# Mixture b's projections read in token order, and the sample's dilated keys kept by residue of four, in a hybrid encoder layer

## The chip, the cores and the metric

One core of a Trainium2 chip runs the whole program. The metric is the device time of one execution in microseconds; lower is better. Three runs of the kernel before took 2401.13, 2403.4 and 2403.99 us; their median is 2403.4 us.

## What is computed

One layer of a bidirectional encoder runs on two requests that share the weights: a prompt of 512 tokens and a sample of 1024, both of width 1024.

```python
x = layer_norm(x)
# token_mixer
q, k, v of a and b = split(x @ w_in)          # 2 x 8 heads of 64
oa = dilated_mixture_attention(rotary(qa), rotary(ka), va)  # windows (128, 1), (512, 4), (2048, 16), merged by lse
ob = neighbourhood_attention(qb, kb, vb, rpb) # tokens as a grid of rows x 64; window 8 x 16, bias by offset
x = layer_norm(ALPHA * x + concat(rmsnorm(oa), rmsnorm(ob)) @ w_out)
x = layer_norm(ALPHA * x + cross_attention(x, mem))   # 4 heads of 256, 256 memory tokens
x = layer_norm(ALPHA * x + relu(x @ w_up)**2 @ w_down)
```

Everything is fp32. The kernel splits each operand of a product into a high part that TensorE multiplies fast and a rest, and adds three products (hi x hi, hi x lo, lo x hi).

## The kernel before

The stages follow one another: keys and values of the memory and the first layer norm (to about 112 us), the prompt's mixture a (112 to 219) and b (219 to 349), the sample's mixture a (349 to 603) and b (603 to 829), then `w_out`, cross-attention and the MLP of both requests to the end. The normalised activations stay in SBUF transposed, features on partitions, as tiles of 8 x 512 tokens: `x0h`/`x0l` are the prompt's high and low parts, `x1` and `x2` the two groups of the sample.

`mixer(r, fill)` (L258) does the mixtures of one request. For each of 4 pairs of heads, `pair_ab` (L595 on) makes the queries and keys of the first head for each group of 512 tokens, the values of both heads, then the attention of the first head, the queries and keys of the second, and its attention. A projection (`proj`, L271) is 8 k-tiles x 3 products = 24 matmuls of 128x512 by `mm3` (L125 to 130) into a PSUM bank `pj`. For mixture b the moving operand is read group by group of the 8-column grid (`p (r g c) -> p g r c`), in runs of 8 tokens, so that the product comes out in the order in which neighbourhoods are compact.

In mixture a, `qk_a` (L335) applies the rotary table (DVE L342 to L344, POOL L345), splits the result (ACT L346, DVE L347), and `stack` (L327 to 333) moves queries and keys by six DMAs on SP's queue into a tile `hd`, where one partition half holds high and the other low parts. In mixture b, `qk_b` (L350 to 365) evacuates PSUM straight into `hd`, with the 1/8 of the scores in the queries, and two DMAs (L364, L365) duplicate the keys to the other half.

The attention of half a head (4 blocks of 128 queries) is a generator, `unit` (L420): scores by two matmuls for each block (L450, L451), bias and row maximum on DVE (L430, `soften`), exponential on ACT (L434); then transposes (L476) and their split (L479, L480); then the product with the values (L492) and ACT's evacuation (L498); then the transposes back (L502) and the sum of halves (L505). `push` and `step` advance the units as a pipeline, one step for each new unit. The sample's mixture a (`attn_a1`, L532) has two units of local blocks (keys 64 before to 64 after) and two of dilated blocks, whose queries and keys are read at stride 4 (`cols(..., 4)`).

The order in which each engine runs its instructions is written out by the framework's scheduler, which works from estimated costs; the engines themselves run in order and wait on semaphores. Tiles come from rotating slots: `gb` has two buffers of 1024 values (mask tables, bias windows), `kv` two, `qt` two. The padded bias table of mixture b, `RB`, is built in DRAM in the first stage (L244 to 251).

Of the kernel before, what the change touches and what calls it, by code (L numbers as in the profile page):

```python
# [36 lines left out]
def tile_encoder_layer(ctx: ExitStack, tc: tile.TileContext, d, outs):  # L37
# [10 lines left out]
    vs = [dr.tile([4, P, 2, 2, NMEM], F32, name=f"vs{i}") for i in range(2)]  # L48
    RB = dr.tile([8, 31, 8, 40], F32, name="RB")
# [197 lines left out]
    rp = d["rpb"]  # L247
    for cq in range(8):
        S.dma_start(RB[:, 8:23, cq, 8:32],
                    bass.AP(tensor=rp.tensor, offset=rp.offset + 14 * 31 + 7 - cq,  # L250
                            ap=[[465, 8], [-31, 15], [1, 24]]))
# [6 lines left out]
    def mixer(r, fill):  # L258
# [12 lines left out]
        def proj(w, g, is_b):  # L271
            o = bank("pj")
            rh, rl = ([x[:, k] for k in range(8)] for x in xg[g])
            if is_b:
                rh, rl = ([a.rearrange("p (r g c) -> p g r c", r=8, g=8) for a in q] for q in (rh, rl))
            mm3(o, w[0], w[1], rh, rl)
            return o

# [48 lines left out]
        def stack(hd, sh, sl, tt):  # L327

            qs, k1, k2 = hd
            for o, x, w in ((slice(0, 64), sh, sl), (slice(64, P), sl, sh)):  # L330
                S.dma_start(f32(qs[o, tt]), f32(x[0:P:2]))
                S.dma_start(f32(k1[o, tt]), f32(x[1:P:2]))
                S.dma_start(f32(k2[o, tt]), f32(w[1:P:2]))

        def qk_a(hd, w, g):  # L335
            o = proj(w, g, False)
# [11 lines left out]
            stack(hd, sh, sl, tt)  # L348

        def qk_b(hd, w, g):  # L350
            o = proj(w, g, True)
            qs, k1, k2 = hd
            lo, hi = slice(0, 64), slice(64, P)
            if r:
                part = lambda a: a.rearrange("p (g x) -> p g x", g=8)[:, :, g * 64:(g + 1) * 64]
                o = o.rearrange("p (g x) -> p g x", g=8)
            else:
                part = lambda a: a
            A.activation(part(qs[lo]), o[lo], AF.Copy, scale=0.125)
            A.activation(part(k2[hi]), o[hi], AF.Copy)  # L360
            V.scalar_tensor_tensor(part(qs[hi]), o[lo], 0.125, f32(part(qs[lo])), op0=ALU.mult, op1=ALU.subtract)
            V.tensor_sub(part(k1[hi]), o[hi], f32(part(k2[hi])))
            if g == ng - 1:
                S.dma_start(f32(k1[lo]), f32(k2[hi]))  # L364
                S.dma_start(f32(k2[lo]), f32(k1[hi]))  # L365
# [9 lines left out]
        def v_proj(v, chunk, pair, is_b):  # L375
# [10 lines left out]
            if is_b and r:  # L386
                vt = slot("kv")
                for g in range(ng):
                    o = proj(w, g, is_b)
                    A.activation(vt.rearrange("p (g x) -> p g x", g=8)[:, :, g * 64:(g + 1) * 64],  # L390
                                 o.rearrange("p (g x) -> p g x", g=8), AF.Copy)
                for k in range(2):
                    v_trans(v[k], [vt[:, c * P:(c + 1) * P] for c in range(4 * k, 4 * k + 4)])
                return
            pad = is_b or r
            last = None
            for g in range(ng):
                o = proj(w, g, is_b)
                vt = slot("kv", 640)
                A.activation(vt[:, 64:576], o, AF.Copy)  # L400
# [19 lines left out]
        def unit(hd, v, h, blocks, norm=None, then=None):  # L420


            qs, k1, k2 = hd
            st = sb.tile([P, 16], F32, name="st", bufs=4)
# [3 lines left out]
            def soften():  # L428
                for i, so, p, bias in todo:
                    V.tensor_tensor_reduce(out=p, in0=so, in1=bias, scale=1.0, scalar=LOWEST, op0=ALU.add,  # L430
                                           op1=ALU.max, accum_out=st[:, 8 + i:9 + i])
                    nm, den = st[:, 2 * i + 1:2 * i + 2], st[:, 2 * i:2 * i + 1]
                    V.tensor_scalar(nm, st[:, 8 + i:9 + i], -1.0, None, op0=ALU.mult)  # L433
                    A.activation(p, p, AF.Exp, bias=nm, accum_out=den)  # L434
# [97 lines left out]
        def attn_a1(hd, v, h, tab, hg):  # L532
            for j in range(2):
                bl = []
                for b in range(4 * j, 4 * j + 4):
                    lead, n = (64, 192) if b == 0 else (0, 192) if b == 7 else (0, 256)
                    bl.append((cols(b * P, P), cols(b * P - 64 + lead, n), tab[:, lead:lead + n], n, lead, 256,
                               (b, b + 1 if b < 7 else "tail")))
# [3 lines left out]
                push(unit(hd, v, h, bl, then=then))  # L542
# [35 lines left out]
        def attn_b(hd, v, h, j, bt, ob, then):  # L578
# [11 lines left out]
            push(unit(hd, v, h, bl, norm=ob, then=then))  # L590
# [40 lines left out]
        for is_b in (False, True):  # L631
            tab = tables(is_b)
            for pair in range(4):
# [542 lines left out]
```

## Time and profile before

| | |
|---|---|
| median of three runs | 2403.4 us |
| the profiled execution | 2400.22 us |
| its span | 2398.4 us |
| instructions in the span | 33111 |
| mean granted TensorE clock | 0.991 |

The profile shows one execution. PE is TensorE's matmuls, PEld its weight loads, DVE is VectorE, ACT ScalarE, POOL GpSimd and SP SyncE, which here issues DMAs; SPq marks SP's DMA queue. A row of a timeline gives the start, the recorded time and the instruction, with the idle time before it and what ended it in brackets. Matmuls overlap: the recorded time of one is longer than the distance to the next. "out<-in" are tile names; `hd<-qt` is a DMA from a tile `qt` into `hd`.

### The profile page before, as it was taken

The numbers are of one execution on the slowest core, as the hardware profiler recorded it, in microseconds if no ns is written. First come the engines' busy times: TensorE is split into PE (matmuls) and PEld (weight loads), VectorE is DVE, ScalarE is ACT, GpSimd is POOL, SyncE is SP. The second block draws the span as 40 slices with busy tenths as digits, with TensorE's granted clock in tenths as the row PEclk, the third lists the DMA queues.
The fourth block names the chain that finished last, engine by engine and source line by source line (L and its number), as shares of the span: only waits on it lengthen the run. The fifth ranks groups of instructions, "written<-read, shape, count | busy, mean of one in ns | idle before, by whom it ended". The sixth has DMA issues, their size and how long they took to land. (4 is left out here: it accounts for less than half of the span.)

```text
span 2398.4 us, 33111 instructions
## 1 busy us (share of the span) xinstructions
PE 2313.8 (96%) x11128; PEld 1911.1 (80%) x11128; DVE 1599.5 (67%) x3304; ACT 1028.7 (43%) x2200; POOL 906.0 (38%) x820
## 2 busy tenths in 40 slices
PE   8989999999999999999989999999999999999987
PEld 6877778988888787877868877878888888888865
DVE  6256545666656677668566487767766696686987
ACT  4346644655545544433233333333354322344443
POOL 7555442212234114533244354555541324213142
PEclk9999999999999999999999999999999999999998
DMA  9666345445435543436335444444489999959762
GB/s 323 203 189 178 89 104 136 116 111 120 103 92 128 174 136 98 127 106 198 101 106 175 123 150 150 122 145 137 160 222 210 207 236 241 212 130 199 196 162 73
DMA packets 389210, 370.99 MB, mean 155 GB/s; under 512 B 71984, under 2 KB 301360, under 8 KB 389040
## 3 DMA queue, kind: packets, MB, share of 16 engines
q1 hardware_dynamic: 346032, 335.31, 47.6%
q0 software_dynamic: 43008, 33.56, 9.9%
q8 instruction: 88, 1.44, 0.3%
q14 instruction: 82, 0.67, 0.1%
HBM read 290.75 MB, written 52.97 MB: 143 GB/s over the span
## 5 line engine op out<-in xcount | busy, mean ns | idle before, releaser
L106 POOL TENSOR_TENSOR wl<-wraw,wh 128x512 fp32r<-128x512 f32 x80 | 105.9, 1338 | 183.5 <-ACT wh L105 167.3
L434 ACT ACTIVATE q<-q,st 128x256 f32<-128x256 f32 (+3 forms) x256 | 138.3, 545 | 75.0 <-DVE st L433 72.1
L975 ACT ACTIVATE wh<-q 128x512 fp32r<-128x512 f32 x176 | 110.0, 625 | 132.7 <-DMA q<-in_w_up_dram 84.4
L976 DVE TENSOR_TENSOR wh<-q,wh 128x512 fp32r<-128x512 f32 x176 | 126.3, 720 | 56.8 <-ACT wh L975 56.8
L480 DVE TENSOR_TENSOR pt<-t,pt 128x512 fp32r<-128x512 f32 x160 | 105.3, 670 | 86.8 <-ACT pt L479 86.2
L960 POOL DMA_DIRECT2D q<-in_w_up_dram x64 | 84.1, 1463 | 182.2 <-DVE h L1013 74.8
L298 POOL TENSOR_TENSOR wl<-wraw,wh 128x256 fp32r<-128x256 f32 x128 | 94.2, 759 | 152.6 <-ACT wh L297 145.7
L913 POOL TENSOR_TENSOR wl<-pt,wh 128x512 fp32r<-128x512 f32 x64 | 91.6, 1451 | 119.0 <-ACT wh L912 118.7
L960 POOL DMA_DIRECT2D q<-in_w_down_dram x64 | 56.4, 956 | 203.4 <-DMA q<-in_w_down_dram 92.2
L479 ACT ACTIVATE pt<-t 128x512 fp32r<-128x512 f32 x160 | 89.4, 582 | 87.3 <-PE o L492 83.8
L106 POOL TENSOR_TENSOR wl<-qt,wh 128x512 fp32r<-128x512 f32 x64 | 101.7, 1609 | 51.6 <-ACT wh L105 43.7
L492 PE MATMUL o<-pt,tok 128*128 128x256 f32 (+3 forms) x560 | 114.0, 314 | 5.8 <-ACT q L498 4.1
L118 POOL TENSOR_TENSOR wl<-wraw,wh 128x512 fp32r<-128x512 f32 x48 | 62.3, 1314 | 127.8 <-ACT wh L117 127.8
L926 DVE TENSOR_TENSOR tok<-tok,t 128x512 f32<-128x512 f32 x124 | 82.8, 679 | 37.3 <-PE t L130 37.3
L130 PE MATMUL pj<-x20h,wl 128*128 128x512 f32 x256 | 101.1, 395 | 2.7 <-POOL wl L106 2.4
L926 DVE TENSOR_TENSOR tok<-tok,s 128x512 f32<-128x512 f32 x124 | 83.8, 679 | 29.7 <-PE s L130 29.5
L128 PE MATMUL pj<-x20h,wh 128*128 128x512 f32 x256 | 100.5, 393 | 1.1 <-ACT wh L105 1.0
L129 PE MATMUL pj<-x20l,wh 128*128 128x512 f32 x256 | 100.0, 390 | 0.0
L1055 ACT ACTIVATE wh<-wraw 128x512 fp32r<-128x512 f32 (+2 forms) x96 | 53.1, 557 | 106.9 <-issue 45.5
L476 PE MATMUL t<-ident,q 128*128 128x128 f32 x624 | 95.3, 274 | 2.8 <-ACT q L434 1.4
L105 ACT ACTIVATE wh<-wraw 128x512 fp32r<-128x512 f32 x80 | 48.0, 627 | 104.1 <-DMA wraw<-in_w_xq_dram 27.2
L492 PEld LDWEIGHTS o<-pt,tok 128*128 128x128 f32 x560 | 83.4, 192 | 11.3 <-ACT q L498 6.3
(489 smaller groups left out, 7601.0 us busy)
## 6 DMA issues: line engine op xcount, KB each, us to landing
q<-in_w_up_dram SPq DMA_DIRECT2D x128, 256.0 KB
q<-in_w_down_dram SPq DMA_DIRECT2D x128, 256.0 KB
wraw<-in_w_in_dram SPq DMA_DIRECT2D x96, 256.0 KB
qt<-in_w_up_dram SPq DMA_DIRECT2D x32, 512.0 KB
pt<-in_w_down_dram SPq DMA_DIRECT2D x32, 512.0 KB
q<-in_w_up_dram POOLq DMA_DIRECT2D x64, 256.0 KB, 8.2
q<-in_w_down_dram POOLq DMA_DIRECT2D x64, 256.0 KB, 6.0
sa<-kv SPq DMA_DIRECT2D x28, 512.0 KB
```

The source lines that it names most:

```text
L106: G.tensor_sub(wl[:, sl], r, f32(wh[:, sl]))
L128: T.matmul(out, lh[k], rh[k], start=(k == 0), stop=False, skip_group_check=True)
L129: T.matmul(out, lh[k], rl[k], start=False, stop=False, skip_group_check=True)
L130: T.matmul(out, ll[k], rh[k], start=False, stop=(k == n - 1), skip_group_check=True)
L434: A.activation(p, p, AF.Exp, bias=nm, accum_out=den)
L476: T.transpose(t[:, x:x + P], p, ident)
L480: V.tensor_sub(lo[:, 0:x], t[:, 0:x], f32(hi[:, 0:x]))
L492: T.matmul(o[:, q0:q0 + n], v(c, h), part[:, x:x + n], start=(done == 0 and part is hi), stop=(done == total - 1 and part is lo), skip_gro ...
L926: V.tensor_add(x, x, q)
L960: G.dma_start(out, src, accum_op=ADD)
L975: A.activation(dst[0], x, AF.Copy)
L976: low.tensor_sub(dst[1], x, f32(dst[0]))
```

## The change

Four things change. `proj` reads the tokens of mixture b in their own order, and the evacuations (ACT and DVE in `qk_b`, ACT in `v_proj`) read PSUM by group and write the same places as before. The factor 1/8 of mixture b moves from the queries into the exponential's scale, and the bias table is multiplied by 8 on its way to `RB`, through SBUF and a new DRAM tile `rp`. In the sample's mixture a, `stack` first copies the high keys (ACT) and the low keys (POOL) into a tile `perm` ordered by residue of four, and the key DMAs move those, 64x4x128 in place of 64x512, so that keys of one residue lie side by side in `hd`; the queries stay as they were. Dilated scores then read keys contiguously, local scores read them in four runs, and the local `soften` reads its mask and writes its result at stride 4, which puts the scores back in token order. `perm` lives in the second buffer of `gb`.

```diff
@@ dram tiles, first stage @@
+    rp = dr.tile([8, 15, 31], F32, name="rp")
...
-    rp = d["rpb"]
+
+    z = slot("tok", 465)
+    S.dma_start(z[0:8], d["rpb"][0].rearrange("h r c -> h (r c)"))
+    V.tensor_scalar(z[0:8], z[0:8], 8.0, None, op0=ALU.mult)
+    S.dma_start(rp.rearrange("h r c -> h (r c)"), z[0:8])
     for cq in range(8):
         S.dma_start(RB[:, 8:23, cq, 8:32],
-                    bass.AP(tensor=rp.tensor, offset=rp.offset + 14 * 31 + 7 - cq,
+                    bass.AP(tensor=rp.tensor, offset=rp[0].offset + 14 * 31 + 7 - cq,
                             ap=[[465, 8], [-31, 15], [1, 24]]))
@@ mixer @@
-        def proj(w, g, is_b):
+        def proj(w, g):
             o = bank("pj")
             rh, rl = ([x[:, k] for k in range(8)] for x in xg[g])
-            if is_b:
-                rh, rl = ([a.rearrange("p (r g c) -> p g r c", r=8, g=8) for a in q] for q in (rh, rl))
             mm3(o, w[0], w[1], rh, rl)
             return o
+        def by_group(a):
+            return a.rearrange("p (r g c) -> p g r c", r=8, g=8)
+        def grouped(a, g):
+            if r:
+                a = a.rearrange("p (g x) -> p g x", g=8)[:, :, g * 64:(g + 1) * 64]
+                return a.rearrange("p g (r c) -> p g r c", r=8)
+            return a.rearrange("p (g r c) -> p g r c", r=8, g=8)
...
+        def by_residue(a):
+            return a.rearrange("p (x q) -> p q x", q=4)
+        def residues(a):
+            return a.rearrange("p (q x) -> p q x", q=4)
-        def stack(hd, sh, sl, tt):
+        def stack(hd, sh, sl, g):
             qs, k1, k2 = hd
-            for o, x, w in ((slice(0, 64), sh, sl), (slice(64, P), sl, sh)):
+            tt = slice(g * 512, (g + 1) * 512)
+            kh, kl = sh, sl
+            if r:
+                kh, kl = perm
+                A.activation(residues(kh), by_residue(f32(sh)), AF.Copy)
+                G.tensor_copy(residues(kl), by_residue(f32(sl)))
+                kh, kl = residues(kh), residues(kl)
+                k1, k2 = (residues(k)[:, :, g * P:(g + 1) * P] for k in (k1, k2))
+            else:
+                k1, k2 = k1[:, tt], k2[:, tt]
+            for o, x, y, z in ((slice(0, 64), sh, kh, kl), (slice(64, P), sl, kl, kh)):
                 S.dma_start(f32(qs[o, tt]), f32(x[0:P:2]))
-                S.dma_start(f32(k1[o, tt]), f32(x[1:P:2]))
-                S.dma_start(f32(k2[o, tt]), f32(w[1:P:2]))
+                S.dma_start(f32(k1[o]), f32(y[1:P:2]))
+                S.dma_start(f32(k2[o]), f32(z[1:P:2]))
...
         def qk_b(hd, w, g):
-            o = proj(w, g, True)
+            o = proj(w, g)
...
-            A.activation(part(qs[lo]), o[lo], AF.Copy, scale=0.125)
+            o = by_group(o)
+            part = lambda a: grouped(a, g)
+            A.activation(part(qs[lo]), o[lo], AF.Copy)
             A.activation(part(k2[hi]), o[hi], AF.Copy)
-            V.scalar_tensor_tensor(part(qs[hi]), o[lo], 0.125, f32(part(qs[lo])), op0=ALU.mult, op1=ALU.subtract)
+            V.tensor_sub(part(qs[hi]), o[lo], f32(part(qs[lo])))
...
@@ v_proj @@
-                    A.activation(vt.rearrange("p (g x) -> p g x", g=8)[:, :, g * 64:(g + 1) * 64],
-                                 o.rearrange("p (g x) -> p g x", g=8), AF.Copy)
+                    A.activation(grouped(vt, g), by_group(o), AF.Copy)
...
-                A.activation(vt[:, 64:576], o, AF.Copy)
+                if is_b:
+                    A.activation(grouped(vt[:, 64:576], g), by_group(o), AF.Copy)
+                else:
+                    A.activation(vt[:, 64:576], o, AF.Copy)
@@ unit @@
-        def unit(hd, v, h, blocks, norm=None, then=None):
+        def unit(hd, v, h, blocks, norm=None, then=None, scale=1.0, local=False):
             qs, k1, k2 = hd
+            order, keyed = (by_residue, residues) if local else (lambda a: a, lambda a: a)
...
-                    V.tensor_tensor_reduce(out=p, in0=so, in1=bias, scale=1.0, scalar=LOWEST, op0=ALU.add,
+                    V.tensor_tensor_reduce(out=order(p), in0=keyed(so), in1=order(bias), scale=1.0, scalar=LOWEST, op0=ALU.add,
                                            op1=ALU.max, accum_out=st[:, 8 + i:9 + i])
...
-                    V.tensor_scalar(nm, st[:, 8 + i:9 + i], -1.0, None, op0=ALU.mult)
-                    A.activation(p, p, AF.Exp, bias=nm, accum_out=den)
+                    V.tensor_scalar(nm, st[:, 8 + i:9 + i], -scale, None, op0=ALU.mult)
+                    A.activation(p, p, AF.Exp, bias=nm, scale=scale, accum_out=den)
@@ attn_a1: local=True for the local units @@
-                    bl.append((cols(b * P, P), cols(b * P - 64 + lead, n), tab[:, lead:lead + n], n, lead, 256,
-                               (b, b + 1 if b < 7 else "tail")))
+                    k0 = (b * P - 64 + lead) // 4
+                    bl.append((cols(b * P, P), lambda z, k0=k0, n=n: residues(z)[:, :, k0:k0 + n // 4],
+                               tab[:, lead:lead + n], n, lead, 256, (b, b + 1 if b < 7 else "tail")))
...
-                        bl.append((cols(512 * i + q, P, 4), cols(q, 256, 4),
+                        bl.append((cols(512 * i + q, P, 4), cols(q * 256, 256),
@@ attn_b: scale=0.125; end of mixer @@
             tab = tables(is_b)
+            perm = parts("gb") if r and not is_b else None
```

The scheduler writes a new order. TensorE's rows are the same up to the start of the sample's mixture a, and no row moves in the MLP. Line numbers of the changed kernel are larger: L450/L451 become L481/L482, L128 to L130 L129 to L131, L476 L507, L502 L533, L371 L398, L410 L439, L345 L375, L331 to L333 L361 to L363, L364/L365 L391/L392, L106 L107, L541 L573, L552 L584, L562 L594, L703 L736.

The first place is TensorE in the sample's mixture a, pair 0, between the first head's first local unit and its second. `s<-hd` are scores, `pj<-x2h,wh` a projection, `t<-ident` transposes. Before:

```order
L502 MATMUL t<-ident,q 128x128 x3
L371 MATMUL pj<-ident,kv 128x128 x4
L410 MATMUL pj<-ident,kv 128x128 x4
L502 MATMUL t<-ident,q 128x128
L450 MATMUL s<-hd 128x256 x2
L476 MATMUL t<-ident,q 128x128 x3
L451 MATMUL s<-hd 128x256 x2
L450 MATMUL s<-hd 128x256
L451 MATMUL s<-hd 128x256
```

And now:

```order
L533 MATMUL t<-ident,q 128x128 x4
L398 MATMUL pj<-ident,kv 128x128 x4
L439 MATMUL pj<-ident,kv 128x128 x4
L507 MATMUL t<-ident,q 128x128
L129 MATMUL pj<-x2h,wh 128x512
L130 MATMUL pj<-x2l,wh 128x512
L131 MATMUL pj<-x2h,wl 128x512
```

Seven more such triples follow, and only then `L481 MATMUL s<-hd 128x256`: a whole projection of 24 matmuls has moved ahead of the second group of scores.

The second place is pair 1 in the same stage. TensorE reaches the first scores of the first head (`128x192`), before:

```order
L130 MATMUL pj<-x1h,wl 128x512
L128 MATMUL pj<-x2h,wh 128x512
L129 MATMUL pj<-x2l,wh 128x512
L130 MATMUL pj<-x2h,wl 128x512
L128 MATMUL pj<-x2h,wh 128x512
L450 MATMUL s<-hd 128x192
L450 MATMUL s<-hd 128x256
L129 MATMUL pj<-x2l,wh 128x512
L451 MATMUL s<-hd 128x192
L450 MATMUL s<-hd 128x256
L451 MATMUL s<-hd 128x256 x2
```

And now:

```order
L129 MATMUL pj<-x1h,wh 128x512
L130 MATMUL pj<-x1l,wh 128x512
L131 MATMUL pj<-x1h,wl 128x512
L481 MATMUL s<-hd 128x192
L481 MATMUL s<-hd 128x256
L129 MATMUL pj<-x2h,wh 128x512
L130 MATMUL pj<-x2l,wh 128x512
L131 MATMUL pj<-x2h,wl 128x512
L482 MATMUL s<-hd 128x192
L481 MATMUL s<-hd 128x256
L482 MATMUL s<-hd 128x256 x2
```

The first scores follow the last `x1` matmul at once, where before four `x2` matmuls stood between. Up to the head's second local unit the order before has 23 projection matmuls (20 of `x2`, 3 of `x1`) after the first score, the new one 35 (24 and 11). On POOL the same pair reads, before:

```order
L445 MEMSET q 128x64
L345 TENSOR_TENSOR qt<-qt 128x512
L106 TENSOR_TENSOR wl<-wraw,wh 128x512 x2
L345 TENSOR_TENSOR qt<-qt 128x512 x2
L298 TENSOR_TENSOR wl<-wraw,wh 128x256 x2
L447 MEMSET q 128x64
```

And now:

```order
L375 TENSOR_TENSOR qt<-qt 128x512
L476 MEMSET q 128x64
L355 CAST gb<-qt 128x512
L107 TENSOR_TENSOR wl<-wraw,wh 128x512 x2
L375 TENSOR_TENSOR qt<-qt 128x512
L355 CAST gb<-qt 128x512
L375 TENSOR_TENSOR qt<-qt 128x512
L355 CAST gb<-qt 128x512
```

The copies `L355` of the low keys stand between the rotary sums `L375`, and the weight split `L107` behind the first of them.

The third place is SP's queue at the end of the sample's mixture a. Before:

```order
L541 DMA oas_61<-cpr 128x4x66
L703 DMA qt<-os_59 128x1024
L364 DMA hd<-hd 64x1024
L365 DMA hd<-hd 64x1024
L552 DMA oas_62<-cpr 128x2x66 x4
L562 DMA gb<-RB 128x16x24
```

And now:

```order
L362 DMA hd<-gb 64x4x128
L361 DMA hd<-qt 64x512
L363 DMA hd<-gb 64x4x128 x2
L362 DMA hd<-gb 64x4x128
L736 DMA qt<-os_59 128x1024
L273 DMA gb<-in_c_m_dram 128x896
L391 DMA hd<-hd 64x1024
L392 DMA hd<-hd 64x1024
L584 DMA oas_62<-cpr 128x2x66 x4
L594 DMA gb<-RB 128x16x24
```

The table of mixture b (`in_c_m`), which was loaded before the sample's mixture a began, is now loaded after the last key DMAs and ahead of the key duplicates `L391` and `L392`.

## Rows read from the trace of the kernel before

**Rows 1.** The page: busy time by engine; the chain that ended last.
```profile
PE 2313.8 (96%) x11128; PEld 1911.1 (80%) x11128; DVE 1599.5 (67%) x3304; ACT 1028.7 (43%) x2200; POOL 906.0 (38%) x820
...
PE 36%; DVE 2%; DMA 1%; POOL 1%; issue 1%; ACT 0%; SPq 0%; ACTq 0%; DVEq 0%
```

**Rows 2.** Windows of three stages (window, length, engines' busy us, granted clock, DMA share).
```profile
219.00:349.00 130.00, 125.08 (x651) 100.55 (x650) 64.17 (x209) 75.63 (x199) 59.66 (x94) 0.99 0.37 93
349.00:603.00 254.00, 249.87 (x1467) 223.94 (x1466) 157.51 (x559) 141.44 (x413) 57.06 (x78) 0.99 0.51 122
603.00:829.00 226.00, 225.81 (x1196) 189.30 (x1195) 138.92 (x445) 120.19 (x305) 72.74 (x89) 1.00 0.47 120
```

**Rows 3.** Waits of PE in the sample's mixture a: total, times, longest.
```profile
PE s L450 <- DMA hd<-qt: 3.6, 1, 3.6
```

**Rows 4.** Timeline of PE: a plain projection, first and last matmul (start, us).
```profile
379.19 0.45 PE L128 MATMUL pj<-x2h,wh 128*128 128x512 f32 x1
...
384.49 0.39 PE L130 MATMUL pj<-x2h,wl 128*128 128x512 f32 x1
```

**Rows 5.** Timeline of PE: a projection of the prompt's mixture b, 1st and 23rd.
```profile
291.46 0.47 PE L128 MATMUL pj<-x0h,wh 128*128 128x512 f32 x1
...
297.09 0.43 PE L129 MATMUL pj<-x0l,wh 128*128 128x512 f32 x1
```

**Rows 6.** Timeline of PE: projections of the sample's mixture b, 22 matmuls.
```profile
719.08 0.47 PE L129 MATMUL pj<-x2l,wh 128*128 128x512 f32 x1
...
724.37 0.43 PE L129 MATMUL pj<-x1l,wh 128*128 128x512 f32 x1
```

**Rows 7.** Timeline of PE: local (445) and dilated (453, 454) scores of 128x256.
```profile
445.47 0.28 PE L451 MATMUL s<-hd 128*128 128x256 f32 x1
...
445.72 0.28 PE L451 MATMUL s<-hd 128*128 128x256 f32 x1
...
453.39 0.42 PE L451 MATMUL s<-hd 128*128 128x256 f32 x1
...
453.87 0.42 PE L451 MATMUL s<-hd 128*128 128x256 f32 x1
...
454.37 0.58 PE L450 MATMUL s<-hd 128*128 128x256 f32 x1
```

**Rows 8.** Timeline of PE's weight loads: contiguous queries (445) and strided ones (454).
```profile
445.36 0.19 PEld L451 LDWEIGHTS s<-hd 128*128 128x128 f32 x1
...
454.34 0.31 PEld L450 LDWEIGHTS s<-hd 128*128 128x128 f32 x1
```

**Rows 9.** Timeline of SP: last key DMAs of stacks in pairs 0 and 1.
```profile
372.30 0.58 SPq L333 DMA_DIRECT2D hd<-qt  x1
...
410.07 0.59 SPq L333 DMA_DIRECT2D hd<-qt  x1
...
415.84 0.59 SPq L333 DMA_DIRECT2D hd<-qt  x1
```

**Rows 10.** Timeline of PE: the score groups that these keys release.
```profile
375.44 0.77 PE L450 MATMUL s<-hd 128*128 128x256 f32 x2 [3.58 <-DMA hd<-qt]
...
415.70 0.39 PE L450 MATMUL s<-hd 128*128 128x192 f32 x2
...
421.65 0.40 PE L450 MATMUL s<-hd 128*128 128x256 f32 x2
```

**Rows 11.** Groups by line, sample's mixture a (busy us, mean ns, idle before).
```profile
L430 DVE CUSTOM_DVE_ANT_0 q<-s,gb 128x256 f32<-128x256 f32 (+1 forms) x112 | 40.9, 410 | 14.9 <-PE s L451 14.1
...
L345 POOL TENSOR_TENSOR qt<-qt 128x512 f32<-128x512 f32 x15 | 19.4, 1290 | 84.0 <-DVE qt L344 66.7 <-DMA hd<-qt 17.3
...
L498 ACT ACTIVATE q<-o 128x512 f32<-128x512 f32 x27 | 16.1, 596 | 9.6 <-PE o L492 9.6
```

**Rows 12.** Timeline of SP: the duplicate of keys for mixture b's first head.
```profile
623.67 0.49 SPq L364 DMA_DIRECT2D hd<-hd  x1
```

**Rows 13.** Timeline of PE: mixture b's first scores of the sample.
```profile
645.72 0.36 PE L450 MATMUL s<-hd 128*128 128x256 f32 x1
```

More of the change, by code (lines that the diff above doesn't have):

```diff
@@ L325, in pair_tiles @@
             return hds, v, chunk
-        def stack(hd, sh, sl, tt):
-            qs, k1, k2 = hd
-            for o, x, w in ((slice(0, 64), sh, sl), (slice(64, P), sl, sh)):
+        def by_residue(a):
[3 more added lines that the diff above has]
+        def stack(hd, sh, sl, g):
+            qs, k1, k2 = hd
+            tt = slice(g * 512, (g + 1) * 512)
[9 more added lines that the diff above has]
+            for o, x, y, z in ((slice(0, 64), sh, kh, kl), (slice(64, P), sl, kl, kh)):
                 S.dma_start(f32(qs[o, tt]), f32(x[0:P:2]))
-                S.dma_start(f32(k1[o, tt]), f32(x[1:P:2]))
-                S.dma_start(f32(k2[o, tt]), f32(w[1:P:2]))
+                S.dma_start(f32(k1[o]), f32(y[1:P:2]))
+                S.dma_start(f32(k2[o]), f32(z[1:P:2]))
         def qk_a(hd, w, g):
-            o = proj(w, g, False)
+            o = proj(w, g)
             tt = slice(g * 512, (g + 1) * 512)
@@ L347, in qk_a @@
             V.tensor_sub(sl, t, f32(sh))
-            stack(hd, sh, sl, tt)
+            stack(hd, sh, sl, g)
         def qk_b(hd, w, g):
-            o = proj(w, g, True)
+            o = proj(w, g)
             qs, k1, k2 = hd
             lo, hi = slice(0, 64), slice(64, P)
[L354 to L358, printed above, removed]
-            A.activation(part(qs[lo]), o[lo], AF.Copy, scale=0.125)
+            o = by_group(o)
+            part = lambda a: grouped(a, g)
+            A.activation(part(qs[lo]), o[lo], AF.Copy)
             A.activation(part(k2[hi]), o[hi], AF.Copy)
-            V.scalar_tensor_tensor(part(qs[hi]), o[lo], 0.125, f32(part(qs[lo])), op0=ALU.mult, op1=ALU.subtract)
+            V.tensor_sub(part(qs[hi]), o[lo], f32(part(qs[lo])))
             V.tensor_sub(part(k1[hi]), o[hi], f32(part(k2[hi])))
@@ L388, in v_proj @@
                 for g in range(ng):
-                    o = proj(w, g, is_b)
-                    A.activation(vt.rearrange("p (g x) -> p g x", g=8)[:, :, g * 64:(g + 1) * 64],
-                                 o.rearrange("p (g x) -> p g x", g=8), AF.Copy)
+                    o = proj(w, g)
+                    A.activation(grouped(vt, g), by_group(o), AF.Copy)
                 for k in range(2):
@@ L397, in v_proj @@
             for g in range(ng):
-                o = proj(w, g, is_b)
+                o = proj(w, g)
                 vt = slot("kv", 640)
-                A.activation(vt[:, 64:576], o, AF.Copy)
+                if is_b:
+                    A.activation(grouped(vt[:, 64:576], g), by_group(o), AF.Copy)
+                else:
+                    A.activation(vt[:, 64:576], o, AF.Copy)
                 if pad and last is None:
@@ L536, in attn_a1 @@
                     lead, n = (64, 192) if b == 0 else (0, 192) if b == 7 else (0, 256)
-                    bl.append((cols(b * P, P), cols(b * P - 64 + lead, n), tab[:, lead:lead + n], n, lead, 256,
-                               (b, b + 1 if b < 7 else "tail")))
+                    k0 = (b * P - 64 + lead) // 4
+                    bl.append((cols(b * P, P), lambda z, k0=k0, n=n: residues(z)[:, :, k0:k0 + n // 4],
+                               tab[:, lead:lead + n], n, lead, 256, (b, b + 1 if b < 7 else "tail")))
                 def then(raw, j=j):
                     S.dma_start(oas[0][j * 512:(j + 1) * 512, hg].rearrange("(i p) c -> p i c", p=P), raw)
-                push(unit(hd, v, h, bl, then=then))
+                push(unit(hd, v, h, bl, then=then, local=True))
             for j in range(2):
@@ L589, in attn_b @@
                                (b, b + 1 if b < 3 else "tail")))
-            push(unit(hd, v, h, bl, norm=ob, then=then))
+            push(unit(hd, v, h, bl, norm=ob, then=then, scale=0.125))
         def pair_ab(pair, is_b, tab):
```

## The prediction

> **What bounds the kernel now.** I read the page first: TensorE (PE) is busy for 96% of the span, and in the chain that ended last PE has 36% of the span and no other engine over 2% [rows 1]. The table by stage then shows whether that holds where the change acts: PE is busy 125.08 of 130 us in the prompt's mixture b, 249.87 of 254 in the sample's mixture a and 225.81 of 226 in its mixture b, at a granted clock of 0.99 to 1.00, so the clock has nothing to give. VectorE (DVE), ScalarE (ACT) and GpSimd (POOL) have a third to three quarters of each stage free [rows 2]. The view of waits holds one PE wait of note in the sample's mixture a, 3.6 us for a DMA into `hd` [rows 3]. So a microsecond comes off the end only if PE's own instructions get shorter or that wait goes. PE's timeline tells what one instruction costs: matmuls overlap, so I take the distance between starts, not the recorded duration.
>
> **Projections of mixture b.** A plain 128x512 projection matmul of the sample's mixture a starts every (384.49 - 379.19)/23 = 0.2304 us [rows 4]. The same matmul with the operand read in runs of eight values starts every (297.09 - 291.46)/22 = 0.2559 us in the prompt's mixture b [rows 5] and every (724.37 - 719.08)/21 = 0.2519 us in the sample's [rows 6]. The change leaves the plain read. Count: 4 pairs x 3 projections x 24 matmuls = 288 for the prompt, twice that, 576, for the sample's two groups. Gain: 288 x 0.0255 = 7.3 and 576 x 0.0215 = 12.4, **-19.7 us**. All of it is PE time in stages that PE bounds.
>
> The regrouping moves to the evacuations, which now read PSUM and write SBUF in runs of eight: 4 for each of 8 heads and group (96) and 12 of values, 108. No row shows such an evacuation. From below it is free; from above it doubles, another 0.60 us each by the ACT row [rows 11], and ACT, busy 75.63 of 130 and 120.19 of 226 us [rows 2], takes even the whole 65 us beside PE. I put it at 0. The scale inside Exp adds no instruction, and the table that is multiplied by 8 costs two DMAs and one DVE instruction in the first stage, far ahead of mixture b: 0.
>
> Where PE gets faster, its covers shrink. The sample's mixture b has no idle PE (0.2 us); the prompt's has 4.9, and 7.3 us less work there can uncover between 0 and 7.3. I take **+2**, a quarter, since ACT and DVE are free half of that stage.
>
> **Dilated scores.** Their keys are read at stride 4: 0.24 us from start to start, (453.87 - 453.39)/2, against 0.125 for local scores of the same 128x256, (445.72 - 445.47)/2 [rows 7]. 8 heads x 2 units x 4 blocks x 2 = 128 matmuls lose the stride. The upper bound is thus 128 x 0.115 = 14.7 us. But their stationary operand, the queries, keeps its stride 4, and its weight load takes 0.31 us where a contiguous one takes 0.19 [rows 8]. The load recorded at 454.34 and the start of its matmul, recorded at 454.37 with 0.58 instead of 0.42 us, hence about 0.16 later in truth, lie 0.19 apart [rows 7, 8]. I read this as: a strided load occupies its path for about 0.2 us before the next can follow, and each of these matmuls has a load of its own. So my estimate for the distance afterwards is 0.22 us, and the gain 128 x 0.02 = **-2.6**, between 0 and -14.7.
>
> **Local scores** now read their keys in four runs of 48 or 64. Bounds: 0, and 128 x 0.0255 = 3.3 us if the runs cost what runs of eight cost. Runs this long are nearest to plain: **+0.2**. DVE reads the mask and writes the scores of 64 local blocks at stride 4; even twice 0.41 us each [rows 11] is 26 us more on an engine busy 157.51 of 254 us [rows 2]: 0.
>
> **The wait at the first head.** Before, PE stands 3.58 us until 375.44 because the last key DMA of the second group is issued only at 372.30, 3.1 us earlier [rows 9, 10]. In the changed order 24 matmuls of a projection, 5.5 us, stand ahead of that second score group. The chain to it is longer, too (next part). I take **-2**, between 0 and -3.58.
>
> **The copies by residue.** Each of 16 `stack` calls gets an ACT copy (like the 128x512 ACT row, 0.60 us) and a POOL copy (like `L345`, 1.29; perhaps twice that, 2.6, as its read is strided) [rows 11]; in all 10 to 19 us on ACT and 21 to 42 on POOL, which have 113 and 197 us free in that stage [rows 2]. So the work is hidden, but the latency is not by itself: keys leave for `hd` later. Take pair 1. The last key DMA of its first group is issued at 410.07; by the 3.1 us above it is there at 413.2, and the first score starts at 415.70: 2.5 us of slack. For the second group 415.84 + 3.1 = 418.9 against 421.65: 2.7 [rows 9, 10]. The new order starts the first scores four matmuls sooner (-0.9: slack 1.6) and puts 8 more matmuls in front of the second ones (+1.8: slack 4.5). The copy is late by 1.3 to 2.6; and the buffer is single, so that the second group's copies wait until the first group's key DMAs have been read: 2.6 (copy) + 3.7 (six issues of about 0.6) + 3.1 (landing) = 9.4 us from stack to stack in place of 415.84 - 410.07 = 5.8 [rows 9], 3.6 later. The second group is thus late by 4.9 to 6.2 against 4.5, which is 0.4 to 1.7 us of PE wait in each of pairs 1 to 3, 1.2 to 5.1: **+2**. Queued behind the waiting copies stand, on ACT, the exponentials of the running head, and on POOL two `L107` and the next `L375`; they are part of that price. The pieces of the key DMAs shrink from 2 KB to 512 bytes; no row shows a price for it here, and SP still issues six of them.
>
> **The order on SP.** `perm` takes the second `gb` buffer, so mixture b's table is loaded only when the last key DMAs have read `perm`, and `L391`/`L392` stand behind it. `L364` was issued at 623.67 and the first score that reads its result starts at 645.72 [rows 12, 13]: 22 us of cover for a wait of one landing (3.1 us). 0.
>
> **Sum:** -19.7 + 2 - 2.6 + 0.2 - 2 + 2 = -20.1; against the profiled execution's own 2400.2 us this is 2380.1. That execution lies 3.2 us below the median of the runs shown, so I forecast **2383** for the median. All low ends but that of the dilated scores (it is R1, below) give -19.7 + 0 - 2.6 + 0 - 3.6 + 1.2 = -24.7, 2379; all high ends -19.7 + 7.3 + 0 + 3.3 + 0 + 5.1 = -4.0, 2399, and they hardly fall together.
>
> **Rivals.**
> *Weight loads hide (R1).* Dilated scores fall to 0.125 us and all 14.7 us come off: 2383 - 12.1 = **2371**. For it: loads overlap the matmuls before them. Against: 0.31 us is longer than a whole 0.125 us matmul. [...] Chance 0.15.
>
> *Runs of eight are free (R2).* If the 0.0255 and 0.0215 us come from something else, such as other reads of the same tiles or the stage's traffic, then projections stay as they are and the first two terms fall away: 2400.2 - 2.6 + 0.2 - 2 + 2 = 2397.8, **2401** on the median, no change. [...] Chance 0.07.
>
> *Half given back (R4).* PE runs ahead of the key duplicates and exponentials of mixture b, and half of the 19.7 us turns into waits: 2383 + 9.9 = **2393**. For it: the prompt's stage has no other work to put in, and evacuations get longer in the chain from projection to score. Against: 0.2 us of idle PE in the sample's stage. Chance 0.11.
>
> *The single `perm` buffer chains the stacks (R3), slower.* If the slack that the new order gives is not there, each second score group of all 8 heads waits 6.2 - 2.7 = 3.5 us: 28 us in place of my 2, so 2383 - 2 + 28 = **2409**. It decides from (2408.2 - 2381)/8 = 3.4 us for each head upwards; below that the projections still win. For it: ACT and POOL run in order, so that a copy that waits for a DMA stops the exponentials behind it, too. Against: the second head's stacks are emitted a whole head ahead of their scores, and 35 matmuls instead of 23 now lie between the two groups. Chance 0.07.
>
> **How the numbers follow.** The forecast has 0.60, R1 0.15, R4 0.11, R2 0.07, R3 0.07. A measurement of this kernel can tell about 0.2% (4.8 us) from no change, so "faster" ends at 2398.6 and "slower" begins at 2408.2. Forecast, R1 and R4 are faster, 0.86, less 0.01 for the forecast's own tail. No change gets that 0.01, R2 and 0.01 of R3, whose time is just past the border: 0.09; the rest of R3, 0.06, is slower. The range reaches down to R1, with a few us for its own spread, and up to R4: 2368 to 2397, which leaves out R2, R3 and the tails.
>
> **What would show it.** Right: all projections of mixture b at 0.230 us from start to start; dilated scores at 0.20 to 0.24 with weight loads still at 0.31; no PE wait over 1 us at the first head, and waits of PE for `hd` under 6 us in all of mixture a; evacuations of b up to twice as long with no one waiting. R1 shows as dilated scores at 0.125. R2 shows as projections of b still at 0.25, R4 as PE idle of some 10 us in the two b stages, R3 as ACT or POOL copies that wait for DMAs and PE waits of 3 us for `hd` at most heads. The forecast is wrong if the span of the two b stages does not shrink by 15 us or more.

## The result, and the profile after

Five executions of the changed kernel took 2383.89, 2383.99, 2384.58, 2386.91 and 2394.04 us, median 2384.58; the five of before beside them 2400.26 to 2403.99, median 2401.13. The ratio is 0.9938, with a 95% interval of 0.9921 to 0.9955. The profiled execution took 2383.99 us with a span of 2382.2, 16.2 less than before's. The forecast was 2383.

The page of the changed kernel, beside [rows 1]:

```profile
PE 2293.0 (96%) x11128; PEld 1903.7 (80%) x11128; DVE 1614.3 (68%) x3305; ACT 1044.8 (44%) x2216; POOL 930.9 (39%) x836
```

PE is busy for 20.8 us less; DVE, ACT and POOL for 14.8, 16.1 and 24.9 us more. Three landmarks on PE cut the span into stages: the first projection of the prompt's mixture b, the first of the sample and the last mixer score. Before (start, us recorded):

```profile
218.77 0.41 PE L128 MATMUL pj<-x0h,wh 128*128 128x512 f32 x1
...
349.98 0.48 PE L128 MATMUL pj<-x1h,wh 128*128 128x512 f32 x1
...
843.43 0.28 PE L451 MATMUL s<-hd 128*128 128x256 f32 x1
```

And after:

```profile
219.70 0.40 PE L129 MATMUL pj<-x0h,wh 128*128 128x512 f32 x1
...
344.49 0.48 PE L129 MATMUL pj<-x1h,wh 128*128 128x512 f32 x1
...
824.28 0.28 PE L482 MATMUL s<-hd 128*128 128x256 f32 x1
```

| stretch | before | after | difference |
|---|---|---|---|
| start to the prompt's mixture b | 218.77 | 219.70 | +0.9 |
| prompt's mixture b | 131.20 | 124.80 | -6.4 |
| sample's mixtures a and b | 493.45 | 479.79 | -13.7 |
| the rest, to PE's last matmul | 1544.96 | 1548.00 | +3.0 |

The mixers gave 20.1 us, the sum of the forecast; 3.9 were lost outside them. To see of what the 13.7 are made, I added up, for each kind of matmul between the landmarks, the time from its start to the next start (any wait of the next matmul is in it): projections 279.8 before, 268.6 after (-11.2); scores 74.2 and 71.4 (-2.8); all others together +0.3, in which the old wait of 3.6 us is gone and new ones are added.

Part of the 13.7 is not the change's. In before's profile the clock was low right behind the wait for `hd` that ended at 375.44 [rows 10]:

```profile
375.40:378.80 3.40, 3.36 (x16) 3.39 (x17) 1.70 (x8) 0.00 (x0) 0.00 (x0) 0.50 0.23 58
```

From there to the next projection at 379.19 [rows 4] PE took 3.75 us. The run with the projections alone (below) has the same matmuls behind its own wait for `hd`, at a clock of 1.00, and takes 2.21 us:

```profile
371.69 0.49 PE L472 MATMUL s<-hd 128*128 128x256 f32 x2 [2.35 <-DMA hd<-qt]
...
373.90 0.44 PE L129 MATMUL pj<-x2h,wh 128*128 128x512 f32 x1
```

So about 1.5 of the 13.7 us are a low clock in before's one profile.

The projections of mixture b, prompt (23 matmuls) and sample (22), against [rows 5, 6]:

```profile
290.42 0.48 PE L129 MATMUL pj<-x0h,wh 128*128 128x512 f32 x1
...
295.50 0.39 PE L130 MATMUL pj<-x0l,wh 128*128 128x512 f32 x1
...
703.80 0.48 PE L130 MATMUL pj<-x2l,wh 128*128 128x512 f32 x1
...
708.66 0.39 PE L130 MATMUL pj<-x1l,wh 128*128 128x512 f32 x1
```

(295.50 - 290.42)/22 = 0.231 and (708.66 - 703.80)/21 = 0.231 us: the plain price of [rows 4]. The evacuations by group cost nothing: 0.684 us (DVE) and 0.581 us (ACT) here, 0.684 and 0.584 before; those of the values take 0.587 us in both. ACT and DVE, group by line, sample's mixture b of the changed kernel:

```profile
L388 DVE TENSOR_TENSOR hd<-pj,hd 64x512 fp32r<-64x512 f32 x16 | 10.9, 684 | 11.1 <-ACT hd L387 10.8
...
L386 ACT ACTIVATE hd<-pj 64x512 fp32r<-64x512 f32 x16 | 9.3, 581 | 7.4 <-PE pj L131 7.3
```

Dilated scores with contiguous keys (timeline of PE, against [rows 7]):

```profile
445.90 0.48 PE L481 MATMUL s<-hd 128*128 128x256 f32 x1
446.22 0.39 PE L482 MATMUL s<-hd 128*128 128x256 f32 x1
446.45 0.40 PE L481 MATMUL s<-hd 128*128 128x256 f32 x1
446.68 0.40 PE L482 MATMUL s<-hd 128*128 128x256 f32 x1
```

From the second on they stand 0.23 us apart; over all such scores with a dilated score before and behind them, the mean went from 0.237 to 0.234 us, which is 0.4 us for 128 of them. The first one behind other work gained more. Its distance to the next is 0.32 here, and it was 0.40 before, from this start to the 453.39 of [rows 7]:

```profile
452.99 0.58 PE L450 MATMUL s<-hd 128*128 128x256 f32 x1
```

Summed from start to next start, all 128 dilated scores took 33.6 us before and 31.8 now: the contiguous key operand bought 1.8 us, where both operands contiguous will bring 14.6 (below).

Waits of PE in the sample's mixture a of the changed kernel (us in total, times, longest), against [rows 3]:

```profile
PE t L507 <- ACT q L465: 3.0, 2, 2.6
PE s L481 <- DVE st L461: 1.2, 2, 0.7
PE s L481 <- DMA hd<-gb: 0.2, 1, 0.2
```

The wait for `hd` is down from 3.6 to 0.2 us, but waits of 4.2 us for ACT's exponentials and DVE's bias step stand in its place, 3.7 of them at the same first head (the two longest here; a third of 0.51 us is behind dilated steps):

```profile
368.89 0.33 PE L507 MATMUL t<-ident,q 128*128 128x128 f32 x1 [2.56 <-ACT q L465]
...
376.33 0.36 PE L481 MATMUL s<-hd 128*128 128x256 f32 x1 [0.68 <-DVE st L461]
```

Groups by line of that stage show what got longer there (busy us, mean ns, idle before):

```profile
L461 DVE CUSTOM_DVE_ANT_1 q<-s,gb 128x256 f32<-128x256 f32 x42 | 24.3, 629 | 7.4 <-PE s L482 7.1
...
L461 DVE CUSTOM_DVE_ANT_0 q<-s,gb 128x256 f32<-128x256 f32 x56 | 20.7, 413 | 0.3
...
L354 ACT ACTIVATE gb<-qt 128x512 fp32r<-128x512 f32 x16 | 18.2, 1141 | 2.3 <-DMA hd<-gb 2.0
...
L355 POOL CAST gb<-qt 128x512 fp32r<-128x512 f32 x15 | 16.6, 1104 | 33.5 <-DVE qt L377 24.9 <-DMA hd<-gb 7.3 <-DVE st L464 1.4
```

The local bias step (`L461`, ANT_1) takes 0.629 us where it took 0.41 [rows 11]; the ACT copy takes 1.14 us (I had taken 0.60) and the POOL copy 1.10 (1.3 to 2.6).

**What was lost outside the mixers.** The granted clock of one stretch in the cross-attention of the changed kernel (window, length, busy us by engine, clock, DMA share):

```profile
1231.60:1237.60 6.00, 6.00 (x18) 5.07 (x19) 2.08 (x3) 1.79 (x3) 0.00 (x0) 0.50 0.42 102
```

The clock is 0.50, and matmuls of 512 columns stand 0.43 us apart, where they stand 0.23 apart once it is back at 0.99. It follows a PE wait of 3.08 us; before, a wait of 3.11 us in the same place was followed by 1.00. Ahead of it the same matmuls come 18.9 us earlier than before, behind it 16.1, so 2.8 us were lost there.

### The profile page after: what moved, and what is told of

It is laid out like the page before. It is cut to its first block, busy times and chain, and to the rows that moved or that the text cites. A ratio compares the mean times of both kernels' runs of the same rounds, so it can differ in the third digit from the quotient of the medians.

```text
span 2382.2 us, 33165 instructions
## 1 busy us (share of the span) xinstructions
PE 2293.0 (96%) x11128; PEld 1903.7 (80%) x11128; DVE 1614.3 (68%) x3305; ACT 1044.8 (44%) x2216; POOL 930.9 (39%) x836
## 5 line engine op out<-in xcount | busy, mean ns | idle before, releaser
L107 POOL TENSOR_TENSOR wl<-wraw,wh 128x512 fp32r<-128x512 f32 x80 | 106.0, 1340 | 173.9 <-ACT wh L106 158.5
L107 POOL TENSOR_TENSOR wl<-qt,wh 128x512 fp32r<-128x512 f32 x64 | 101.7, 1609 | 50.8 <-ACT wh L106 42.8
L131 PE MATMUL pj<-x20h,wl 128*128 128x512 f32 x256 | 101.2, 395 | 2.7 <-POOL wl L107 2.4
L129 PE MATMUL pj<-x20h,wh 128*128 128x512 f32 x256 | 100.6, 393 | 0.3 <-ACT wh L106 0.2
L130 PE MATMUL pj<-x20l,wh 128*128 128x512 f32 x256 | 100.0, 391 | 0.0
L507 PE MATMUL t<-ident,q 128*128 128x128 f32 x624 | 95.2, 273 | 5.0 <-ACT q L465 3.6
L106 ACT ACTIVATE wh<-wraw 128x512 fp32r<-128x512 f32 x80 | 47.7, 626 | 103.5 <-PE pj L131 24.8
L945 ACT ACTIVATE wh<-pt 128x512 fp32r<-128x512 f32 x64 | 36.9, 624 | 122.0 <-PE s L131 103.0
```

The lines of the kernel that those rows point to most:

```text
L107: G.tensor_sub(wl[:, sl], r, f32(wh[:, sl]))
L129: T.matmul(out, lh[k], rh[k], start=(k == 0), stop=False, skip_group_check=True)
L130: T.matmul(out, lh[k], rl[k], start=False, stop=False, skip_group_check=True)
L131: T.matmul(out, ll[k], rh[k], start=False, stop=(k == n - 1), skip_group_check=True)
L507: T.transpose(t[:, x:x + P], p, ident)
```

## The experiments

**The change once more** (no edit).

> The changed kernel once more, for its time beside the parts and for one place: in its first profile the granted clock was 0.50 from 1231.6 to 1237.6 us, behind a PE wait of 3.08 us, and some 2.8 us were lost there. Theory 'chance': the time is 2384 +- 3 us, and the low stretch is absent or stands elsewhere. Rival 'the new order brings it': the same stretch shows 0.50 again.

2384.88 us (median of 6), ratio 0.9925 (0.9912 to 0.9938). At the cross-attention place the clock was not low at that matmul, though PE's wait ahead of it was only 1.77 us this time, so the same wait was not tried there. Instead the clock fell twice in the prompt's mixture b, which now took 128.1 us. PE's wait ahead of the first fall, and the windows of both, in this run:

```profile
309.42 1.15 PE L523 MATMUL o<-pt,tok 128*128 128x256 f32 x8 [1.18 <-ACT q L529]
```

```profile
311.50:314.70 3.20, 3.20 (x9) 2.52 (x8) 0.47 (x4) 1.89 (x9) 2.64 (x4) 0.50 0.21 55
338.80:342.00 3.20, 3.20 (x8) 2.52 (x9) 0.55 (x5) 2.26 (x10) 2.89 (x5) 0.50 0.21 55
```

In the first profile of the same program, the same wait and the window behind it:

```profile
310.06 1.15 PE L523 MATMUL o<-pt,tok 128*128 128x256 f32 x8 [1.18 <-ACT q L529]
```

```profile
309.00:314.00 5.00, 3.62 (x20) 3.09 (x21) 3.43 (x19) 4.79 (x17) 4.66 (x7) 1.00 0.31 88
```

The same instructions behind the same wait of 1.18 us run at 0.50 in one execution and at 1.00 in the other. 'Chance' holds: where the clock falls differs from execution to execution of one program. The chip is not what decides it: the run with contiguous queries (below), whose order on PE is the same in this stage, ran on the same chip as the repeat and took 124.7 us for the prompt's mixture b, at 1.00 throughout. Before's profile has such a place in the prompt's mixture b, too:

```profile
313.00:321.00 8.00, 7.67 (x29) 5.95 (x28) 1.72 (x12) 2.88 (x12) 3.86 (x6) 0.79 0.46 113
```

8 us at 0.79 are 1.7 us lost, so that of the 6.4 us above about 4.7 are the change's. The run with the residue keys alone (below) has before's projections in this stage at a clock of 1.00 throughout, and comes to the same: 129.5 us, against the 124.8 of the changed kernel's first profile.

```profile
220.74:350.27 129.53, 124.79 (x661) 100.48 (x660) 64.19 (x209) 77.07 (x200) 60.03 (x95) 1.00 0.37 94
```

```profile
219.70:344.49 124.79, 118.71 (x661) 99.43 (x660) 64.32 (x209) 77.26 (x201) 60.31 (x95) 1.00 0.38 97
```

**The projections alone.**

```diff
# after, with stack, attn_a1 and the local soften as before
-            perm = parts("gb") if r and not is_b else None
-                        bl.append((cols(512 * i + q, P, 4), cols(q * 256, 256),
+                        bl.append((cols(512 * i + q, P, 4), cols(q, 256, 4),
```

> The change without the residue keys: projections of mixture b in token order, keys of the sample's mixture a stored and read as before (stride 4 in dilated scores). Theory 'projections alone' (dilated scores stay at 0.234 us because the strided weight load bounds them): as fast as the whole change, ratio to before 0.993, 2384 +- 2 us, and PE waits 3 to 4 us for hd at the first head as before. Rival 'the keys give 4 us' (as in the forecast, -2.6 and -2): 2388 to 2389 us. Rival 'the copies cost' (the 4.4 us of new PE waits for ACT and DVE in mixture a are a loss): 2379 to 2381 us.

2385.64 us, ratio 0.9927 (0.9915 to 0.9939), beside 0.9925 for the whole change on the same chip. PE waits in the sample's mixture a, longest row:

```profile
PE s L472 <- DMA hd<-qt: 2.6, 2, 2.4
```

The old wait for `hd` is back (2.6 us, a little less than the 3 to 4 expected), and the time is the same. The first theory holds. The stage says so, too: from the first projection of the sample to its last score PE took 480.7 us here, of which 3.4 at a clock of 0.50, against 479.8 and 478.9 us in the two profiles of the whole change, both at 1.00.

**The residue keys alone.**

```diff
# after, with the read of before
+            if is_b:
+                rh, rl = ([a.rearrange("p (r g c) -> p g r c", r=8, g=8) for a in q] for q in (rh, rl))
```

> The residue keys alone, projections of mixture b read in runs of eight as before (the 1/8 stays in the exponential). Theory 'projections alone': within 2 us of before, 2399 to 2403 us, projections at 0.252 us, dilated scores at 0.234 us. Rival 'the keys give 4 us': 2395 to 2397. Rival 'the copies cost': 2403 to 2406.

2400.74 us (12 runs), ratio 0.9987 (0.9975 to 1.0). It lies in the first theory's 2399 to 2403, but the median is 2.2 us below the 2402.97 of before on this chip, and 0.9987 is 3.1 us, between that theory and the rival of 4: by this run alone, anything from 0 to 0.25% (6 us) is in the keys. With the run before it, whose time and stage leave them next to nothing, the gain is in the projections, to within the few us that these runs can tell.

**Queries contiguous, too.**

```diff
-                        bl.append((cols(512 * i + q, P, 4), cols(q * 256, 256),
+                        bl.append((cols(512 * i + q * P, P), cols(q * 256, 256),
```

> The whole change, but the dilated scores take 128 neighbouring queries as stationary operand instead of every fourth, so that this load is contiguous, too; other queries are scored, the amount of work is the same. Theory 'strided weight load bounds': the load falls from 0.31 to 0.19 us, the distance of dilated scores from 0.234 to about 0.12, and 128 x 0.115 = 14.7 us come off: 2369 to 2372 us. Rival 'something else holds the dilated scores' (such as PSUM or the scores of 256 columns themselves): the distance stays at 0.23 and the time at 2384.

2376.89 us, ratio 0.9892 (0.9878 to 0.9905). Scores of a dilated block on PE, and a weight load between them:

```profile
445.89 0.28 PE L481 MATMUL s<-hd 128*128 128x256 f32 x1
446.01 0.28 PE L482 MATMUL s<-hd 128*128 128x256 f32 x1
```

```profile
445.78 0.19 PEld L481 LDWEIGHTS s<-hd 128*128 128x128 f32 x1
```

0.12 us apart, load 0.19: with contiguous keys, the stride of the queries did hold the dilated scores. By the sums from start to start they lost 12.8 us against the repeated change (31.8 to 19.0), but the time only 8.0, which misses the theory's 2369 to 2372: PE now waits more for ACT and DVE (the sums of transposes and value transposes rose by 5.6).

**Queries contiguous, keys strided.**

```diff
-                        bl.append((cols(512 * i + q, P, 4), cols(q, 256, 4),
+                        bl.append((cols(512 * i + q * P, P), cols(q, 256, 4),
```

This stands on the kernel with the projections alone.

> Projections in token order, keys as before the change (stride 4 as moving operand of the dilated scores), but 128 neighbouring queries as stationary operand; other queries are scored, the amount of work is the same. The run with plain queries and residue keys had 0.119 us between dilated scores and 2377 us. Theory 'only the load's stride costs': 0.12 us here, too, and 2377 to 2379 us. Rival 'either stride alone costs the whole': 0.23 us and 2385. Between them: 0.15 to 0.2 us, 2380 to 2383.

2381.33 us, ratio 0.9915 (0.9895 to 0.9935). Timeline of PE and of its weight loads:

```profile
450.38 0.43 PE L472 MATMUL s<-hd 128*128 128x256 f32 x1
450.61 0.43 PE L473 MATMUL s<-hd 128*128 128x256 f32 x1
```

```profile
450.39 0.21 PEld L473 LDWEIGHTS s<-hd 128*128 128x128 f32 x1
```

0.23 us again, with loads of about 0.2: the rival 'either stride alone costs the whole' has the distance. The median lies 4 us below its 2385, which the interval reaches, and most of that is in the scores all the same: the first dilated score behind other work is 0.28 us from the next (0.40 with both strides), and all 128 together take 30.6 us, 3.0 less than with strided queries. The four cases of operands now read (median distance of dilated scores one behind the other; in brackets the sum of all 128, from start to next start):

| us | keys at stride 4 | keys contiguous |
|---|---|---|
| queries at stride 4 | before: 0.235 (33.6) | the change: 0.234 (31.8) |
| queries contiguous | 0.233 (30.6) | 0.119 (19.0) |

**Queries kept by residue**, a version that computes the same: two more DMAs for each stack, into columns 3200 to 4095 of `hd`; the eighth block (q = 3, second half) keeps its stride.

```diff
+                n = 512 - g * P
+                for o, y in ((slice(0, 64), perm[0]), (slice(64, P), perm[1])):
+                    S.dma_start(f32(hd[3][o, g * 512:g * 512 + n]), f32(y[0:P:2, 0:n]))
...
+                        m = 4 * i + q
+                        bl.append(((cols(P * m, P), hd[3]) if m < 7 else cols(512 * i + q, P, 4), cols(q * 256, 256),
```

> The whole change, and the dilated queries kept by residue as well: two more DMAs for each stack put them into the 896 free columns of hd, so 7 of 8 dilated blocks read both operands contiguously, the eighth its queries at stride 4; the output is the reference's. Theory: 112 of 128 dilated scores at 0.12 us, -11 us in the scores, of which waits for ACT and DVE take a third as with plain queries: 2376 to 2379 us. Rival 'the issues': two more issues of 0.6 us for each of 16 stacks put the keys off, PE waits for hd grow to 6 us and more: 2382 to 2386.

2385.18 us (2379.97 to 2389.88), ratio 0.993 (0.9912 to 0.9948). Dilated scores lost 9.4 us against the repeated change, of the 11 expected, and the time did not move. PE waits in the sample's mixture a, the three largest:

```profile
PE s L486 <- DVE st L465: 3.5, 7, 0.7
PE pj L402 <- ACT kv L433: 1.9, 1, 1.9
PE t L512 <- ACT q L469: 1.8, 2, 1.3
```

Neither expectation had this: not the key DMAs, but DVE's release of the two score banks and ACT hold PE up once it is that fast. All PE waits for these two come to 8.2 us in the stage, where the repeated change has 3.0, and the transposes and products with the values, summed from start to start, rose by 8.2 us.

> Residue queries once more, on the chip of the run with the mask: its six times before lay between 2380 and 2390 us, wider than others. Theory 'waits eat the gain': again within 2 us of the changed kernel, ratio to before 0.992 to 0.994. Rival 'clock drops hid a gain': ratio 0.989 to 0.991, as with plain queries.

2384.05 us, ratio 0.9915 (0.9898 to 0.9932). The two medians are 2385.2 and 2384.1; 'waits eat the gain' fits the time, though the ratio lies between the two ranges given. A gain over the change of up to about 5 us is not excluded by these intervals.

**The local mask by residue, too**, on top of the last version: one ACT copy of the mask per stage, so that DVE reads it in the order of the scores.

```diff
-                    V.tensor_tensor_reduce(out=order(p), in0=keyed(so), in1=order(bias), scale=1.0, scalar=LOWEST, op0=ALU.add,
+                    V.tensor_tensor_reduce(out=order(p), in0=keyed(so), in1=bias, scale=1.0, scalar=LOWEST, op0=ALU.add,
```

> Queries kept by residue in 7 of 8 dilated blocks, as before, and the local mask kept by residue, too (one ACT copy for the whole stage), so that DVE reads both inputs of the local bias step in one order and only its output is strided. With residue queries alone, PE waited 3.5 us in seven places for this step, which takes 0.63 us where a plain one takes 0.42. Theory 'the strided mask is the price': 0.45 to 0.5 us, PE waits for DVE fall to 1 to 2 us: 2 us less than residue queries alone, 2380 to 2383. Rival 'the strided output is the price': still 0.63 us and the same time, 2383 to 2386.

2383.05 us, ratio 0.9917 (0.9902 to 0.9931). The bias step of 128x256, local (42) and dilated (56) in one row:

```profile
L467 DVE CUSTOM_DVE_ANT_0 q<-s,gb 128x256 f32<-128x256 f32 x98 | 44.1, 506 | 8.1 <-PE s L489 8.0
```

98 x 0.506 less 56 x 0.415 leaves 0.627 us for a local one, as before the edit, and PE still waits 3.8 us in eight places for DVE: the price is not the mask's stride, so it is the output's or that of reading the scores in four runs; which of them was not tried. No version that computes the same beats the change clearly.

**Run lengths.**

```diff
+            if run[0]:
+                rh, rl = ([a.rearrange("p (r g c) -> p g r c", g=8, c=run[0]) for a in q] for q in (rh, rl))
```

> The whole change, with the projections of mixture b reading their tokens in runs of 1, 2, 4 and 8 (prompt, pairs 0 to 3) and of 2, 4, 16 and 32 (sample); the products come out in another token order, the number of matmuls is the same. Theory 'each new run costs a fixed stall' (0.0215 us for 64 runs of 8, 0.34 ns a run): 0.240 us for runs of 16, 0.235 for 32, 0.273 for 4, 0.315 for 2, 0.40 for 1. [...]

2447.29 us (one run). Rows of PE for runs of 1 (218.85), 4 (324.44), 8 (365.17) and 2 (640.46), first and last of 7, 7, 12 and 12 matmuls, and the granted clock of the first and the last of these:

```profile
218.85 0.61 PE L131 MATMUL pj<-x0h,wl 128*128 128x512 f32 x1
...
221.44 0.61 PE L131 MATMUL pj<-x0h,wl 128*128 128x512 f32 x1
...
324.44 0.41 PE L130 MATMUL pj<-x0l,wh 128*128 128x512 f32 x1
...
325.92 0.41 PE L130 MATMUL pj<-x0l,wh 128*128 128x512 f32 x1
...
365.17 0.42 PE L131 MATMUL pj<-x0h,wl 128*128 128x512 f32 x1
...
367.99 0.43 PE L130 MATMUL pj<-x0l,wh 128*128 128x512 f32 x1
...
640.46 0.61 PE L129 MATMUL pj<-x2h,wh 128*128 128x512 f32 x1
...
645.20 0.61 PE L131 MATMUL pj<-x2h,wl 128*128 128x512 f32 x1
```

```profile
217.00:222.00 5.00, 5.00 (x13) 2.39 (x12) 2.15 (x4) 2.29 (x6) 3.29 (x5) 1.00 0.55 158
...
640.00:645.50 5.50, 5.50 (x14) 2.68 (x13) 3.33 (x10) 0.58 (x1) 0.55 (x1) 1.00 0.31 90
```

| run of fp32 values | 1 | 2 | 4 | 8 | 16 | 32 | plain |
|---|---|---|---|---|---|---|---|
| median distance, us | 0.431 | 0.431 | 0.247 | 0.2545 | 0.233 | 0.236 | 0.227 |

The theory falls: it gives 0.40 us for single values, 0.315 for runs of 2 and 0.273 for runs of 4, where 0.431, 0.431 and 0.247 were measured. A run of 2 costs as much as single values, at a granted clock of 1.00; and from 4 on the price does not go with the number of runs (128 of them 0.247 us, 64 of them 0.2545). The runs of one group lie eight run lengths apart, so that length and distance grow together here; which of the two sets the price was not separated.

## Why the prediction was right, point by point

**The forecast** was 20 us off the time; the medians give 16.6 and, in the repeat, 18.1. What carried it is the first term, and the runs show it: a projection matmul of mixture b went from 0.25 to 0.231 us, and the projections alone have a ratio of 0.9927.

**Projections**: right in kind, a little high in size. -19.7 less a cover of 2 was forecast. 11.2 us (of 12.4) came off in the sample and 6.4 in the prompt, the latter with 1.7 us of a low clock in before's profile; at a clock of 1.00 the prompt's projections went from 74.5 us (the run with the keys alone) to 68.5, 6.0 of the forecast 7.3 (its 0.2559 was read off one projection; the median over the stage is 0.251), and 1.1 us of that went into longer PE waits (4.7 to 5.8). The evacuations at 0 were right. R2 is out: projections went from 0.25 to 0.231 us, and the change without the keys has the gain.

**Dilated scores**: -2.6 was forecast, 1.8 came, but not in the way forecast. I had read a distance of 0.22 us out of one load's start, and it is 0.234 (0.4 us in all); the rest came at the first score behind other work, which the forecast did not ask about. That the queries' stride would hold it was right: with the queries contiguous as well, the load falls from 0.31 to 0.19 us and the distance to 0.119. That a strided load occupies its path for about 0.2 us was my estimate from two rows; no run shows it by itself. What was not asked is whether the keys' stride holds the distance by itself. It does: either stride alone keeps 0.23, with the keys' stride at a load of only 0.21. R1 did not come: the queries' stride remained, and with it loads of 0.31 to 0.33 us.

**Local scores** in runs of 64 have a median distance of 0.118 us, where it was 0.119 before: +0.2 was forecast, nothing came.

**The first head's wait** for `hd` went, from 3.6 us to 0.2 (forecast -2), and **the copies** did not put off the keys, where 1.2 to 5.1 us of PE wait for `hd` were forecast and R3 needed 28. But PE stands at that head as long as before: 3.7 us, for ACT and DVE (2.56 of it in one place, 1.40 there in the repeat). So the sign "no PE wait over 1 us at the first head" did not come true. The steps that failed are a zero and a price: "DVE reads the mask and writes the scores ... 0" (0.63 us a step, and PE waits 0.7 us for it), and the ACT copy at 0.60 us (1.14). That these two brought the rest of the 4.2 us of new waits, too, is argued from the rows and not shown: the order of PE and of the other engines changed in the same place. That "the clock has nothing to give" failed, too: a low clock behind the old wait cost before's profile 1.5 us.

In the sum the errors cancel. -2.4 was forecast for all that the keys do, and the sample's mixers gave 13.7 - 11.2 = 2.5 beside the projections: 3.4 of the old wait, 1.8 of the dilated scores and 1.5 of the clock, less 4.2 of new waits. Without the clock that is 1.0 us for the keys, and the run without the keys had the same time, so that this net is within what the runs can tell from nothing.

**Half given back (R4)** did not come: PE waits 0.3 us in the sample's mixture b until 808 us, and 3.9 from there to its last score; before had 0.2 until 829 us, and 3.4.

**Outside**: 3.9 us in the first profile; 2.8 of them are one fall of the clock, which the repeated run has elsewhere (it lost 1.5 us outside). So the 20.1 us of the mixers, of which 3.2 are before's low clock, and the profile's 2383.99 beside 2383 agree with the forecast by luck, to a few us; that the ratio over all runs is 0.9925 to 0.9938 is not luck.

## What to carry to other kernels

Where PE bounds a stage, read the distance between starts of one matmul form in two layouts: that difference times the count gave 19.7 us here, of which 17 came, and moving the reorder to the evacuation was free (0.684 us on DVE before and after, 0.584 and 0.581 on ACT). Making one operand of a matmul contiguous was worth 1.8 or 3.0 us here while the other was strided, and both together 14.6; test both at once before paying copies for one. A wait that goes can come back under another name at the same place: look there for every releaser, not only for the old one. And a stage that is bound by PE at 98% can have another engine right behind it: 9 us off PE's scores brought no time.

## What was not expected of the hardware

A moving operand in runs of 2 fp32 values costs 0.431 us for 512 columns, the same as single values, and runs of 4 cost 0.247 (plain 0.227), all at a granted clock of 1.00. A stride of 4 in the stationary operand alone or in the moving operand alone gives the same 0.23 us for 256 columns, and both together hardly more (0.235), where neither gives 0.119. The granted clock fell to 0.50 for about 3 to 6 us behind PE waits of 1.2 to 3.6 us in some executions, and stayed at 1.00 behind the same wait of 1.18 us of the same program in another.
